# Keys and queries stored by class, the first norm's sums by parts, and halves for the last five output tiles

## The chip, the core and the metric

The kernel runs on one core of a Trainium2 chip. The core has five engines with queues of their own, and each runs its instructions in the order of its queue: TensorE (PE in the profile, PEld for its weight loads), VectorE (DVE), ScalarE (ACT), GpSimd (POOL) and SyncE (SP), which here issues nearly all DMAs. Semaphores are all that ties the queues together. TensorE writes to PSUM (8 banks of 128x512 f32); the other operands lie in SBUF.

The metric is the device time of one execution in microseconds; the median of three runs stands for a kernel.

## The reference

One decoder block over 512 tokens of width 1024, in float32. A vector `c` gives nine modulation vectors (shift, scale and gate for each of three sub-layers); around a token-mixing layer stand two feed-forward layers, and an RMSNorm ends it.

```python
mod = cond @ w_ada[l] + b_ada[l]                  # cond = silu(c), nine parts of 1024
u = modulate(rmsnorm(h, g_norm_ffn1[l]), sh1, sc1)
h = h + 0.5 * gt1 * swiglu(u, w_ffn1_in[l], w_ffn1_out[l])
u = modulate(rmsnorm(h, g_norm_mix[l]), sh2, sc2)
h = h + gt2 * token_mixing(u, cos, sin, w_in[l], w_pool[l], ...)
u = modulate(rmsnorm(h, g_norm_ffn2[l]), sh3, sc3)
h = h + 0.5 * gt3 * swiglu(u, w_ffn2_in[l], w_ffn2_out[l])
return rmsnorm(h, g_final)

def swiglu(u, w_in, w_out):                       # inner width 2816
    a, b = jnp.split(u @ w_in, 2, axis=-1)
    return (jax.nn.silu(a) * b) @ w_out

def token_mixing(u, cos, sin, w_in, ...):
    p, q, k, v, gate_logits = jnp.split(u @ w_in, cuts, axis=-1)
    y_pool = multiscale_pool(p, w_pool, pool_scale)
    q, k = apply_rope(q, ...), apply_rope(k, ...)  # 12 heads of 64, in 3 groups
    for gi, (window, dilation) in enumerate(((128, 1), (512, 4), (2048, 16))):
        o, lse = dilated_window_attention(q[gi], k[gi], v[gi], window // dilation, dilation)
    y_attn = sum of the groups' o, weighted by softmax of their lse
    merged = g_pool * (y_pool @ w_pool_branch) + g_attn * (y_attn @ w_attn_branch)
    return merged @ w_out
```

With dilation 4, token t attends to t, t - 4, t - 8 and so on: the tokens fall into four classes (t modulo 4) of 128 tokens, and queries meet only keys of their class. With dilation 16 the kernel uses the same four classes and a mask.

## The kernel before

Activations lie transposed: eight tiles `H[k]` of 128 channels x 512 tokens. A matmul of full float32 accuracy is made of three in the faster type fp32r (`mm3`, L321): weights and activations are each split into a high and a low part, and hi·uh, hi·ul and lo·uh are summed into one bank. Plain f32 matmuls, which the profile shows as two records each, serve for sums, spreads, scores and transposes.

Weights come by a list that is planned ahead (`plan`): SyncE loads chunks of 128x1024 or less into three buffers `raw` (in part of the run also `X`); `split_hi` (L257) writes the high half of a chunk to the ring `whi` on ScalarE (L280), `split_lo` (L286) the low half to `wlo` on VectorE (L292), and frees the buffer. `look(ahead)` (L301) splits so many chunks ahead of the one in use, `take` hands out the next. While `held` is set, `look` does nothing and chunks are split one by one. All queues are in the order of the Python program (`manual_schedule`).

The modulation is worked out on VectorE: `ada_fetch` loads a 128x1024 tile of `w_ada`, and `ada_do` (L341) multiplies it with `cond` and sums along the row into one column of `mod` (L346). `bg` does one such tile beside a piece of TensorE's work, and `bg_fetch` loads `ada_depth` tiles ahead.

The stages, in order:

- `startup` (L1336): loads, cond, squares of `H[k]` on ScalarE (L1369) summed pairwise into two tiles by VectorE (L1371), then across channels by one-column matmuls (L1377), root (L1378), reciprocal (L1381), and a spread of the result over 128 partitions by matmuls with the identity (L1386). `warm` (L1362) issues matmuls whose results are not used. `norm_t` (L420), `norm_u` (L427) and `norm_b` (L443) make a norm's scaled tile, its high part UH and its low part UL. Then the first four pairs of feed-forward 1, all eight k, in eight banks (L1421 to L1425).
- `ffn` (L788): pairs of tiles in and silu, or two pairs at once with seven products instead of eight (`duo`), and the output matrix in five parts. In the last part each output tile m gets its residual update (L856) and its squares (`sumsq`, added on GpSimd, L396). In feed-forward 1 the rotary tables' steps (`trig`, L888) are taken from `todo`, four for each m; the last step runs the sines on ScalarE (L912 to L914).
- `out_tail` (L475) does the last tiles of feed-forward 1 (m = 4 to 7) and of the mixing layer (m = 5 to 7) by halves A and B of 256 tokens: all tiles for A, then all for B. During B, `stats_t` (L398, L406) and `spread` (L413, L416) finish A's norm, and `norm_steps` gives the next stage's UH and UL, so that `head` can start on A.
- `mix` (L1113): projections, rotary embedding (`rope`, L918: four products of 128x512, L924, four add/subtracts of 64x512, L928 and L929), attention in units (kind, n, pair of heads). `at_prep` (L958) makes zero-padded queries for two heads, `at_scores` the scores (L975 and L977 for dilation 1, L981 for a class), the maximum on VectorE (L993) and Exp on ScalarE (L998), `at_turn` the transposes (L1010), `at_values` the values (L1033). `hooks` places these pieces between the k steps of projections. `pool_diff` is GpSimd's.
- `merge_out` (L1230): per m, two gate projections with four `bg`, then the merge of the branches into MH and ML (L1258 to L1262); then w_out.
- `ffn2`, and `out_end` (L514): the last five tiles in two parts of 384 and 128 tokens, with the final norm's statistics, products (`final`, L528, on VectorE and GpSimd) and stores (L531).

Classes are taken by a step of four in the free dimension:

```python
return ((0,), slice(n * P, n * P + P)) if kind == 0 else ((1, 2), slice(n, T, 4))
```

Of the kernel before, what the change touches and what calls it, by code (L numbers as in the profile page):

```python
# [136 lines left out]
class Kernel:  # L137
# [203 lines left out]
    def ada_do(self, j, n=1):  # L341
        t, mod = self.adat.pop(j), self.mod[:, j:j + 1]
        for i in range(n):
# [4 lines left out]
            if i:  # L348
                self.nc.vector.tensor_tensor(mod, mod, o, op=OP.add)
        if self.ada_free is not None:  # L350
            self.ada_free.append(t)
# [75 lines left out]
    def norm_u(self, n, k, hs, t):  # L427
# [3 lines left out]
        if n == 0:  # L431
            u = self.Xall.rearrange("p (a h k t) -> p a h k t", a=2, h=2, k=4)[:, k // 4, :, k % 4, :]
            act(u, t.rearrange("p (h t) -> p h t", h=2), AF.Identity, bias=S, scale=1.0)
# [41 lines left out]
    def out_tail(self, ms, ksrc, gate, nxt, squares):  # L475
# [7 lines left out]
        for h, hs in enumerate((A, Bh)):  # L483
            for m in ms:
# [10 lines left out]
                for i, (hi, lo, uh, ul) in enumerate(ks):  # L495
                    if h == 1 and m == ms[1] and i == 3:
                        self.stats_t(self.B[6], A)
                    if h == 1 and m == ms[2] and i == 1:
                        self.spread(self.B[6], A)
                        self.place_u(nxt)  # L500
                        step = self.norm_steps(nxt, A)
                    self.mm3(bank[:, hs], hi, lo, uh[:, hs], ul[:, hs], i == 0, i == len(ks) - 1)
                s = squares(m)[:, :HT]
                self.tail_step(m, hs, bank, gate, s)
                self.split_lo()
                if h == 1:
                    self.held = starts[m + 1]
                    if step:
                        step(1 if m != ms[-1] else 3)
                nc.vector.tensor_tensor(self.acc[:, hs], self.acc[:, hs], s, op=OP.add)  # L510
# [3 lines left out]
    def out_end(self, ms, ksrc, gate):  # L514
# [3 lines left out]
        M = nc.tensor.matmul  # L518
        tiles = {}
        A, Bh = slice(0, 3 * P), slice(3 * P, T)  # L520
# [12 lines left out]
        rA, rB = self.B[6], self.B[7]  # L533
        for h, hs in enumerate((A, Bh)):
            for m in ms:
# [6 lines left out]
                if h and m == ms[2]:  # L542
                    self.stats_t(rA, A)
                if h and m == ms[-1]:
                    self.spread(rA, A)
                    nc.scalar.activation(self.R[:, A], rA[:, A], AF.Copy)
                    for i in range(4):
                        final(g, i, A, self.R)
                        if i % 2:
                            store(i - 1, i + 1, A, nc.sync)  # L550
                    final(v, 4, A, rA)
                for i, (hi, lo, uh, ul) in enumerate(tiles[m]):
                    self.mm3(bank[:, hs], hi, lo, uh[:, hs], ul[:, hs], i == 0, i == len(tiles[m]) - 1)
                s = self.tp.tile([P, T], F32, name="ut")[:, :hs.stop - hs.start]
# [6 lines left out]
        self.stats_t(rB, Bh, (self.acc[:, Bh], s), lambda: final(v, 5, A, rA))  # L561
        scaled(ms[-1], Bh)
        store(4, 6, A, nc.scalar)
        self.spread(rB, Bh)
        for i in (6, 7):
# [925 lines left out]
```

## Time and profile before

| | us |
|---|---|
| three runs: median (lowest, highest) | 1047.0 (1045.74, 1047.56) |
| the profiled execution | 1041.36 |
| its span, first to last instruction | 1039.5 |
| TensorE idle within the span | 19.2 |
| from TensorE's last tile matmul to the end of the span | 9.8 |

Granted clock 0.995 on average. The span cut into 40 equal slices, in tenths of busy time (page, part 2):

```profile
PE   8999999999999999999999999999999999999996
DVE  6968879789786777777356677467787777667753
ACT  5443253525434543333324233453356254353542
PEclk9999999999999999999999999999999999999998
DMA  8857356455524223222044775421344234251202
```

TensorE has work in every slice. VectorE follows with some 7 tenths; where it drops, around the attention and at the end, TensorE is not waiting for it. DMA is heavy at the start and where the modulation is loaded. A busy TensorE says nothing of how fast its matmuls follow each other: the groups by line do. Means are of durations, which overlap; the distance between starts is what counts.

```profile
L683 PE MATMUL bank<-UH,whi 128*128 128x256 f32 x512 | 141.6, 277 | 0.0
L292 DVE TENSOR_TENSOR wlo<-raw,whi 128x1024 fp32r<-128x1024 f32 (+2 forms) x150 | 177.7, 1188 | 65.3 <-ACT whi L280 65.0
```

The columns: line, engine, operation, out<-in with the shapes, count | busy us, mean ns of one | idle time before, and what ended most of it.

### The profile page before, as it was taken

The numbers are of one execution on the slowest core, as the hardware profiler recorded it, in microseconds if no ns is written. First come the engines' busy times: TensorE is split into PE (matmuls) and PEld (weight loads), VectorE is DVE, ScalarE is ACT, GpSimd is POOL, SyncE is SP. The second block draws the span as 40 slices with busy tenths as digits, with TensorE's granted clock in tenths as the row PEclk, the third lists the DMA queues.
The fourth block names the chain that finished last, engine by engine and source line by source line (L and its number), as shares of the span: only waits on it lengthen the run. The fifth ranks groups of instructions, "written<-read, shape, count | busy, mean of one in ns | idle before, by whom it ended". The sixth has DMA issues, their size and how long they took to land.

```text
span 1039.5 us, 15505 instructions
## 1 busy us (share of the span) xinstructions
PE 1020.3 (98%) x6346; PEld 920.2 (89%) x6346; DVE 747.4 (72%) x1073; ACT 435.9 (42%) x635; POOL 37.6 (4%) x37
## 2 busy tenths in 40 slices
PE   8999999999999999999999999999999999999996
PEld 6888898989899899889988887998899899998996
DVE  6968879789786777777356677467787777667753
ACT  5443253525434543333324233453356254353542
POOL 0000000000000100008000000100000000000001
PEclk9999999999999999999999999999999999999998
DMA  8857356455524223222044775421344234251202
GB/s 309 283 203 242 123 202 200 164 165 174 169 71 132 91 76 102 62 61 82 11 157 158 229 237 197 130 61 61 102 152 133 80 102 142 82 157 61 93 16 82
DMA packets 42505, 139.14 MB, mean 134 GB/s; under 512 B 4673, under 2 KB 7617, under 8 KB 42434
## 3 DMA queue, kind: packets, MB, share of 16 engines
q1 hardware_dynamic: 41490, 137.42, 40.8%
q8 instruction: 50, 0.82, 0.3%
q10 hardware_dynamic: 944, 0.72, 0.2%
q14 instruction: 21, 0.17, 0.1%
HBM read 135.49 MB, written 2.64 MB: 133 GB/s over the span
## 4 chain that ended last, share of the span: by engine, by line
PE 84%; DVE 7%; DMA 3%; ACT 3%; issue 2%; SPq 0%; DVEq 0%; ACTq 0%
PE bank L325 14%; PE bank L324 14%; PE bank L323 14%; PE bank L683 10%; PE bank L685 10%; PE bank L684 10%; DMA ada<-wada 3%; DVE ada L346 2%; DVE wlo L292 1%; PE bank L1421 1%; PE bank L1425 1%; PE bank L1423 1%; PE bank L981 1%; PE bank L1033 1%; PE bank L1212 1%
## 5 line engine op out<-in xcount | busy, mean ns | idle before, releaser
L292 DVE TENSOR_TENSOR wlo<-raw,whi 128x1024 fp32r<-128x1024 f32 (+2 forms) x150 | 177.7, 1188 | 65.3 <-ACT whi L280 65.0
L280 ACT ACTIVATE whi<-raw 128x1024 fp32r<-128x1024 f32 (+2 forms) x150 | 150.3, 1008 | 49.4 <-DVE raw L228 36.9
L323 PE MATMUL bank<-UH,whi 128*128 128x512 f32 (+1 forms) x432 | 159.3, 369 | 2.0 <-ACT UH L430 2.0
L324 PE MATMUL bank<-UL,whi 128*128 128x512 f32 (+1 forms) x432 | 155.1, 359 | 0.3
L325 PE MATMUL bank<-UH,wlo 128*128 128x512 f32 (+1 forms) x432 | 154.9, 359 | 0.2 <-DVE wlo L292 0.2
L325 PE MATMUL bank<-HI,wlo 128*128 128x512 f32 (+3 forms) x406 | 147.9, 364 | 0.4 <-DVE wlo L292 0.4
L323 PE MATMUL bank<-HI,whi 128*128 128x512 f32 (+3 forms) x406 | 148.0, 364 | 0.0
L324 PE MATMUL bank<-HK,whi 128*128 128x512 f32 (+3 forms) x406 | 147.8, 364 | 0.0
L683 PE MATMUL bank<-UH,whi 128*128 128x256 f32 x512 | 141.6, 277 | 0.0
L684 PE MATMUL bank<-UL,whi 128*128 128x256 f32 x512 | 141.6, 277 | 0.0
L685 PE MATMUL bank<-UH,wlo 128*128 128x256 f32 x512 | 141.6, 277 | 0.0
L292 DVE TENSOR_TENSOR wlo<-X,whi 128x1024 fp32r<-128x1024 f32 (+1 forms) x87 | 104.4, 1200 | 43.7 <-ACT whi L280 43.5
L683 PE MATMUL bank<-SH,whi 128*128 128x256 f32 x384 | 107.0, 279 | 0.0
L685 PE MATMUL bank<-SH,wlo 128*128 128x256 f32 x384 | 106.9, 278 | 0.0
L684 PE MATMUL bank<-SL,whi 128*128 128x256 f32 x384 | 106.9, 278 | 0.0
L280 ACT ACTIVATE whi<-X 128x1024 fp32r<-128x1024 f32 (+1 forms) x87 | 89.2, 1037 | 29.2 <-DVE X L228 27.4
L683 PEld LDWEIGHTS bank<-UH,whi 128*128 128x128 f32 x512 | 96.1, 188 | 0.3
L684 PEld LDWEIGHTS bank<-UL,whi 128*128 128x128 f32 x512 | 96.1, 188 | 0.3
L685 PEld LDWEIGHTS bank<-UH,wlo 128*128 128x128 f32 x512 | 96.4, 188 | 0.0
L323 PEld LDWEIGHTS bank<-UH,whi 128*128 128x128 f32 x432 | 81.4, 188 | 14.4 <-ACT UH L430 2.4
L325 PEld LDWEIGHTS bank<-UH,wlo 128*128 128x128 f32 x432 | 81.3, 188 | 13.3 <-DVE wlo L292 0.6
L324 PEld LDWEIGHTS bank<-UL,whi 128*128 128x128 f32 x432 | 81.4, 189 | 12.7 <-DVE UL L445 0.7
(222 smaller groups left out, 1752.9 us busy)
## 6 DMA issues: line engine op xcount, KB each, us to landing
ada<-wada SPq DMA_DIRECT2D x47, 512.0 KB, 4.7
raw<-wmix SPq DMA_DIRECT2D x44, 512.0 KB, 3.8
raw<-wf1i SPq DMA_DIRECT2D x34, 512.0 KB, 4.5
raw<-wf2i SPq DMA_DIRECT2D x30, 512.0 KB, 3.5
X<-wf2i SPq DMA_DIRECT2D x14, 512.0 KB, 3.5
cs<-wada SPq DMA_DIRECT2D x12, 512.0 KB, 3.5
AR<-wada SPq DMA_DIRECT2D x12, 512.0 KB, 4.4
raw<-wf2o SPq DMA_DIRECT2D x12, 512.0 KB, 4.0
```

The costliest lines, as they stand in the source:

```text
L280: self.nc.scalar.activation(self.hi[:, y], r[:, x], AF.Copy)
L292: self.nc.vector.tensor_tensor(self.lo[:, y], r[:, x], self.hi[:, y], op=OP.subtract)
L323: M(ps, hi, uh, start=start, stop=False)
L324: M(ps, hi, ul, start=False, stop=False)
L325: M(ps, lo, uh, start=False, stop=stop)
L346: self.nc.vector.scalar_tensor_tensor(t[:, c], t[:, c], 1.0, self.cond[:, c], op0=OP.mult, op1=OP.mult, accum_out=o)
L683: M(o, hi, uh, start=start and p == 0 and k == 0, stop=False, skip_group_check=True)
L684: M(o, hi, ul, start=False, stop=False, skip_group_check=True)
L685: M(o, lo, uh, start=False, stop=k == 3, skip_group_check=True)
L981: M(S[:, o + i * P:o + i * P + P], qz[:, (2 * i + h) * P:(2 * i + h + 1) * P], k[:, toks], start=True, stop=True)
L1033: M(o, pt[:, blk * P:blk * P + P], v, start=i == 0, stop=i == len(srcs) - 1)
L1212: M(b, self.UH[k][:, c::4], hi, start=k == 0, stop=False)
```

## The change

Six edits in one:

1. `rope` gets `classes`: with 4 it writes its results by class, reading the products with step 4; `at_tokens` then takes a contiguous block for dilations 4 and 16 too.
2. `startup`: the squares' sums go into one-column matmuls in three parts (k odd up to 5, k even up to 6, k = 7 alone), the reciprocal stands between the two halves of modulation tile 8, the first weight chunk's high half and UH stand ahead of the copy of the spread, and the warm-ups are other ones. The constants' load moves behind tile 8's.
3. `out_end`: halves of 256 tokens instead of 384 and 128; products and stores are placed anew.
4. `out_tail`: the first norm step right behind the spread, and the low half of a split behind the steps.
5. `ffn`, last part: `look` up to five chunks ahead instead of three, and six trig steps for each m instead of four.
6. `merge_out`: four modulation buffers instead of two, loaded four ahead.

```diff
@@ -338,7 +338,7 @@
         self.adat[j] = t
-    def ada_do(self, j, n=1):
+    def ada_do(self, j, n=1, between=None):
         t, mod = self.adat.pop(j), self.mod[:, j:j + 1]
@@ -347,6 +347,8 @@
                 self.nc.vector.tensor_tensor(mod, mod, o, op=OP.add)
+            elif between:
+                between()
         if self.ada_free is not None:
@@ -424,13 +426,17 @@
         return t
-    def norm_u(self, n, k, hs, t):
+    def norm_x(self, k, hs, t):
+        u = self.Xall.rearrange("p (a h k t) -> p a h k t", a=2, h=2, k=4)[:, k // 4, :, k % 4, :]
+        self.nc.scalar.activation(u, t.rearrange("p (h t) -> p h t", h=2), AF.Identity, bias=self.mod[:, k:k + 1], scale=1.0)
+    def norm_u(self, n, k, hs, t, rest=True):
         S = self.mod[:, 24 * n + k:24 * n + k + 1]
...
         act(self.UH[k][:, hs], t[:, hs], AF.Identity, bias=S, scale=1.0)
-        if n == 0:
-            u = self.Xall.rearrange("p (a h k t) -> p a h k t", a=2, h=2, k=4)[:, k // 4, :, k % 4, :]
-            act(u, t.rearrange("p (h t) -> p h t", h=2), AF.Identity, bias=S, scale=1.0)
+        if n == 0 and rest:
+            self.norm_x(k, hs, t)
         if n == 2 and hs.start:
@@ -499,14 +505,15 @@
                         step = self.norm_steps(nxt, A)
+                        step(0)
                     self.mm3(bank[:, hs], hi, lo, uh[:, hs], ul[:, hs], i == 0, i == len(ks) - 1)
...
                 self.tail_step(m, hs, bank, gate, s)
-                self.split_lo()
                 if h == 1:
...
                         step(1 if m != ms[-1] else 3)
+                self.split_lo()
                 nc.vector.tensor_tensor(self.acc[:, hs], self.acc[:, hs], s, op=OP.add)
@@ -515,9 +522,9 @@
         v, g = nc.vector, nc.gpsimd
-        M = nc.tensor.matmul
         tiles = {}
-        A, Bh = slice(0, 3 * P), slice(3 * P, T)
+        A, Bh = slice(0, HT), slice(HT, T)
+        rA, rB = self.B[6], self.B[7]
         self.held = self.pos
@@ -539,36 +545,39 @@
                         nc.scalar.preload_act_table(AF.Sqrt)
-                if h and m == ms[2]:
-                    self.stats_t(rA, A)
-                if h and m == ms[-1]:
-                    self.spread(rA, A)
-                    nc.scalar.activation(self.R[:, A], rA[:, A], AF.Copy)
-                    for i in range(4):
-                        final(g, i, A, self.R)
-                        if i % 2:
-                            store(i - 1, i + 1, A, nc.sync)
-                    final(v, 4, A, rA)
+                n = len(tiles[m])
                 for i, (hi, lo, uh, ul) in enumerate(tiles[m]):
-                    self.mm3(bank[:, hs], hi, lo, uh[:, hs], ul[:, hs], i == 0, i == len(tiles[m]) - 1)
-                s = self.tp.tile([P, T], F32, name="ut")[:, :hs.stop - hs.start]
+                    if h and m == ms[1] and i == n // 2:
+                        self.stats_t(rA, A)
+                    if h and m == ms[2] and i == n // 2:
+                        self.spread(rA, A)
+                        nc.scalar.activation(self.R[:, A], rA[:, A], AF.Copy)
+                        for j in range(4):
+                            final(g, j, A, self.R)
+                            if j % 2:
+                                store(j - 1, j + 1, A, nc.sync)
+                    self.mm3(bank[:, hs], hi, lo, uh[:, hs], ul[:, hs], i == 0, i == n - 1)
+                s = self.tp.tile([P, T], F32, name="ut")[:, :HT]
                 self.tail_step(m, hs, bank, gate, s)
...
                 v.tensor_tensor(self.acc[:, hs], self.acc[:, hs], s, op=OP.add)
-        self.stats_t(rB, Bh, (self.acc[:, Bh], s), lambda: final(v, 5, A, rA))
+                if h and m in ms[2:4]:
+                    j = 4 + 2 * (m - ms[2])
+                    for x in (j, j + 1):
+                        final(v, x, A, rA)
+                    store(j, j + 2, A, nc.sync)
+        self.stats_t(rB, Bh, (self.acc[:, Bh], s))
         scaled(ms[-1], Bh)
-        store(4, 6, A, nc.scalar)
         self.spread(rB, Bh)
-        for i in (6, 7):
-            final(v, i, A, rA)
-        store(6, 8, A, nc.sync)
-        for i in range(KT):
-            final(v, i, Bh, rB)
-            if i in (2, 5, 7):
-                store({2: 0, 5: 3, 7: 6}[i], i + 1, Bh, nc.sync if i == 5 else nc.scalar)
+        nc.scalar.activation(self.R[:, Bh], rB[:, Bh], AF.Copy)
+        for e, js, queue in ((v, (0, 1), nc.scalar), (g, (2, 3), nc.sync), (v, (4, 5), nc.scalar), (v, (6, 7), nc.scalar)):
+            for j in js:
+                final(e, j, Bh, rB if e is v else self.R)
+            store(js[0], js[1] + 1, Bh, queue)
     def head(self, n, banks, table):
@@ -833,7 +842,7 @@
             def ks(m):
-                self.look()
+                self.look(max(3, min(m + 2, 5)))
                 return [(hi, lo, *hk[k]) for k, (hi, lo) in enumerate(self.take())]
@@ -857,7 +866,7 @@
                     nc.scalar.activation(self.O[m], self.H[m], AF.Copy, scale=self.g(3)[:, m:m + 1])
-                for _ in range(4):
+                for _ in range(6):
                     if self.todo:
@@ -915,7 +924,8 @@
         return todo
-    def rope(self, pa, pb, dst):
+    def rope(self, pa, pb, dst, classes=1):
         v = self.nc.vector
@@ -925,8 +935,10 @@
             cols = slice(T * half, T * half + T)
-            v.tensor_tensor(dst[0:64, cols], t[0][rows], t[1][rows], op=OP.subtract)
-            v.tensor_tensor(dst[64:128, cols], t[2][rows], t[3][rows], op=OP.add)
+            src = [x[rows].rearrange("p (i c) -> p c i", c=classes) for x in t]
+            to = [dst[r, cols].rearrange("p (c i) -> p c i", c=classes) for r in (slice(0, 64), slice(64, 128))]
+            v.tensor_tensor(to[0], src[0], src[1], op=OP.subtract)
+            v.tensor_tensor(to[1], src[2], src[3], op=OP.add)
     def mm_tile(self, hooks=()):
@@ -943,9 +955,10 @@
         kind, n, hp = u
-        return ((0,), slice(n * P, n * P + P)) if kind == 0 else ((1, 2), slice(n, T, 4))
+        return (1, 2) if kind else (0,), slice(n * P, n * P + P)
     def at_prep(self, u):
@@ -1192,7 +1205,7 @@
                     ps = [self.mm_tile(hooks(todo.pop(0), nxt=todo[0] if todo else ())) for s in range(2)]
-                    self.rope(ps[0], ps[1], dst)
+                    self.rope(ps[0], ps[1], dst, 4)
             g23 = [[(1, c, hp) for hp in range(2)] for c in range(4)]
@@ -1231,10 +1244,10 @@
         with tc.tile_pool(name="mb", bufs=1) as mb, tc.tile_pool(name="mw", bufs=6) as mw, \
-                tc.tile_pool(name="mada", bufs=2) as self.adaw:
+                tc.tile_pool(name="mada", bufs=4) as self.adaw:
             MH = [mb.tile([P, T], F32R, name=f"MH{k}") for k in range(KT)]
             ML = [mb.tile([P, T], F32R, name=f"ML{k}") for k in range(KT)]
-            self.ada_stop, self.ada_depth = 72, 2
+            self.ada_stop, self.ada_depth = 72, 4
             self.bg_fetch()
@@ -1344,8 +1357,8 @@
         nc.sync.dma_start(self.vecs, a["vecs"])
+        self.ada_fetch(8, 2)
         nc.sync.dma_start(self.cst, a["cst"][:, :163])
-        self.ada_fetch(8, 2)
         self.fetch(0)
@@ -1361,31 +1374,39 @@
                 M(self.B[5][:, :P], self.ones, x[:, :P], start=True, stop=True)
+        def part(s, first, last):
+            for n in range(4):
+                M(self.B[7][:, n:n + 1], s[:, n * P:(n + 1) * P], self.ones[:, 0:1], start=first and n == 0, stop=last,
+                  skip_group_check=True)
         acc = (self.acc, self.R)
...
             nc.scalar.activation(s, self.H[k], AF.Square)
-            if k > 1:
+            if 1 < k < 7:
                 v.tensor_tensor(acc[k % 2], acc[k % 2], s, op=OP.add)
-            if k < 7:
-                warm(1, self.H[min(k, 3)])
-        for n in range(4):
-            for i in range(2):
-                M(self.B[7][:, n:n + 1], acc[i][:, n * P:(n + 1) * P], self.ones[:, 0:1], start=i == 0, stop=i == 1)
+            if k < 4:
+                warm(2 if k > 1 else 1, self.H[k])
+            elif k in (5, 6):
+                part(acc[k % 2], k == 5, False)
+            elif k == 7:
+                part(s, False, True)
         nc.scalar.activation(self.r4, self.B[7][:, :4], AF.Sqrt, bias=self.eps, scale=1.0 / D)
+        warm(2, self.H[7])
+        g, b1 = self.g(0), self.vecs[:, 8:16]
         self.ada_do(0)
-        self.ada_fin("shift", 0, 1)
-        v.reciprocal(self.r4, self.r4)
-        g, b1 = self.g(0), self.vecs[:, 8:16]
-        v.scalar_tensor_tensor(b1, b1, 1.0, g, op0=OP.add, op1=OP.mult)
+        self.ada_do(8, 2, lambda: v.reciprocal(self.r4, self.r4))
         for n in range(4):
             M(self.B[6][:, n * P:(n + 1) * P], self.r4[:, n:n + 1].to_broadcast([P, P]), self.ident, start=True, stop=True)
-        warm(10, self.acc)
-        self.ada_do(8, 2)
+        warm(6, self.H[7])
+        v.scalar_tensor_tensor(b1, b1, 1.0, g, op0=OP.add, op1=OP.mult)
+        self.ada_fin("shift", 0, 1)
         def scale(k):
@@ -1395,15 +1416,19 @@
         self.Rn = {0: self.B[6]}
+        self.split_hi()
         t = self.norm_t(0, 0, full)
+        self.norm_u(0, 0, full, t, rest=False)
+        self.ada_do(1)
+        self.norm_b(0, 0, full, t)
+        self.split_lo()
         nc.scalar.activation(self.R, self.B[6], AF.Copy)
         self.Rn[0] = self.R
-        self.split(0)
-        self.norm_u(0, 0, full, t)
-        self.norm_b(0, 0, full, t)
+        self.norm_x(0, full, t)
         for k in range(KT):
             if k + 1 < KT:
-                self.ada_do(k + 1)
+                if k:
+                    self.ada_do(k + 1)
                 self.ada_fin("shift", k + 1, k + 2)
```

## What I predicted

> **What bounds the kernel now.** I read the page, then TensorE's waits, then the timeline of each place where TensorE waits or runs thin, then the granted clock by windows.
>
> ```profile
> PE 1020.3 (98%) x6346; PEld 920.2 (89%) x6346; DVE 747.4 (72%) x1073; ACT 435.9 (42%) x635; POOL 37.6 (4%) x37
> ```
>
> TensorE is busy for all but 19.2 of 1039.5 us. So time can come from two sources only: those 19.2 us (start 0 to 7, end 1029.7 to 1039.5, and a few waits), and matmuls that take longer than they need. The waits (us in total, times, longest):
>
> ```profile
> PE bank L323 <- ACT UH L430: 2.0, 2, 1.5
> PE bank L323 <- ACT MH L1261: 1.4, 1, 1.4
> PE bank L406 <- DVE AR L510: 1.1, 1, 1.1
> ```
>
> The slow matmuls, in TensorE's timeline (start, us, what): four records of contiguous keys, and eight of keys taken with step 4.
>
> ```profile
> 407.43 0.60 PE L975 MATMUL bank<-k,qz 128*128 128x128 f32 x4
> 407.79 0.48 PE L323 MATMUL bank<-UH,whi 128*128 128x512 f32 x1
> ...
> 482.60 2.00 PE L981 MATMUL bank<-k,qz 128*128 128x128 f32 x8
> 484.24 0.60 PE L1212 MATMUL bank<-whi,UH 128*128 128x512 f32 x1
> ```
>
> The starts inside such groups stand 0.110 us apart at L975 and 0.227 at L981, the same 128 columns each. The next lines are stretches of the run: busy time of PE, PEld, DVE, ACT and POOL, and then the granted clock (1.00, then 0.50), the DMA's share and GB/s.
>
> ```profile
> 10.97:14.38 3.41, 2.48 (x19) 2.31 (x20) 2.60 (x8) 0.26 (x1) 0.00 (x0) 1.00 1.05 392
> 14.38:17.80 3.42, 3.42 (x19) 3.42 (x18) 2.03 (x8) 1.21 (x3) 0.00 (x0) 0.50 1.04 413
> 359.10:362.50 3.40, 2.25 (x20) 2.08 (x19) 2.35 (x6) 0.99 (x3) 0.00 (x0) 1.00 0.75 196
> ```
>
> A stretch of 3.41 us with mostly one-column matmuls (L1377) was followed by one at half clock; a stretch with 2.25 us of ordinary matmuls was not.
>
> **The change part by part.** Profiled execution: 1041.36 us, span 1039.5. I sum differences and take them from the median of the runs, 1047.0; the profiled one lies 5.6 below it, and I assume the difference stays.
>
> *Keys and queries by class.* The 8 units of L981 lose their step. Now a unit costs: first record 482.60 to next matmul 484.24 is 1.64, and that matmul then holds TensorE 0.44 instead of 0.235, so 1.84. Contiguous: two groups like L975's (0.36 + 0.31 - 0.23 = 0.44 each), 0.88. Eight units: 8 x 0.95 = 7.6 gained. What pays: `rope` reads its products with step 4 in 16 add/subtracts of 64x512 (0.69 each now). The nearest row is the query preparation L958: pitch 0.20 contiguous, 0.245 with step 4 (2.06 for 8), so 0.045 more per 128 elements, 0.18 for 512 with one such input, 0.36 with two: 0.7 to 1.4 per rope. Behind the rope on VectorE stands a unit's maximum, then ScalarE's Exp, then TensorE's transposes; at 455.4 these start about 1.0 us after they could. So 0 to 0.4 shows at each of three ropes. And preparation L958 under GpSimd's work took 4.15 for 8 (489.20), ending 1.4 before its scores; GpSimd would now overlap all of it: 0 to 0.8. I take 0.5 off: **-7.1** (-7.7 to -5.5).
>
> *Startup.* Now: last square 10.80, add 11.67, 16 one-column records to 13.45, root, reciprocal 13.78, spread 14.01 to 15.77, ten warm-ups to 18.89, and L1421 starts there (UH was ready at 18.84). Changed: three parts, 24 records at 0.112, from 10.5 (add of k=5 ends 10.46): 2.7 plus two at half clock gives 13.5. So the parts alone gain nothing: the eight records more eat the earlier start. The modulation half that now stands ahead of the reciprocal (0.68) fits between 12.3 and 13.45. The gain is later: ScalarE no longer has the copy of R (0.50) and the weight's first half (1.04) between norm and UH, and 6 warm-ups replace 10. Spread 14.1; if the clock falls at 14.38 again, spread ends 15.8, norm 16.75, UH 17.5, but twelve warm-up records (ten at 0.214, two at 0.112) end at 18.1. If it does not fall, UH is ready at 16.9. Gain 0.8 or 2.0; the window would again hold mostly one-column matmuls, so I take **-0.9** (-2.0 to -0.3). The next k is covered: VectorE needs 5.32 per k, TensorE 5.6. The constants' DMA moves behind two halves of a modulation tile (0.5 MB, 1.3 us at the 400 GB/s of that time) and lands near 13.2, ahead of the spread.
>
> *Norm behind the spread, first place (feed-forward 1 to mixing).* UH's wait at 367.61 (0.48, and 0.17 of slow first matmul) goes: -0.65. But the other two edits here work on the same engines.
>
> ```profile
> 346.78 0.64 ACT L912 ACTIVATE cs<-cs 128x512 f32<-128x512 f32 x1 [0.43 <-DVE cs L908]
> 349.46 0.96 DVE L292 TENSOR_TENSOR wlo<-X,whi 128x768 fp32r<-128x768 f32 x1 [2.71 <-ACT whi L280]
> 350.34 0.74 DVE L856 SCALAR_TENSOR_TENSOR H<-bank,mod,H 128x512 f32<-128x512 f32 x1
> 360.06 0.41 DVE L510 TENSOR_TENSOR AR<-AR,X 128x256 f32<-128x256 f32 x1
> 360.62 0.58 PE L406 MATMUL bank<-ones,AR 128*128 128x1 f32 x4 [1.15 <-DVE AR L510]
> ```
>
> Now one weight half (341.24) passes ahead of the sines; taking six trig steps at a time puts the sines ahead of it, and `look(4)`, `look(5)` then put two splits ahead of each of the updates L856 of m=2 and m=3. Played through with these durations: trig ends 344.4 to 345.0, sines leave ScalarE at 346.2 to 346.9, two splits, update 2 ends 349.5 to 350.2, its square, two splits (one 1024 wide), update 3 ends 353.7 to 354.9 (now 351.0), square, table load 1.28, and the first half-tile's square only at 356.0 to 356.8 (now 353.8). From there 1.9 per tile: the sum for L406 is ready at 361.6 to 362.9 instead of 360.47. TensorE loses its 0.39 wait for wlo at 354.06 and so stands there from 358.7: 3 to 4 us idle, +1.6 net. After such an idle stretch the clock would fall for 3.41 us, 1.7 more, taken at 1.5. Sum **+2.4** (-2.5 if the sum came in time, to +4). [...]
>
> *Deeper modulation buffers.*
>
> ```profile
> 634.84 1.22 DVE L346 SCALAR_TENSOR_TENSOR ada<-ada,cond 128x1024 f32<-128x1024 f32 x1 [1.50 <-DMA ada<-wada]
> 640.25 0.50 PE L323 MATMUL bank<-MH,whi 128*128 128x512 f32 x1 [1.45 <-ACT MH L1261]
> ```
>
> Per m, VectorE has 10.7 us of work (four modulation tiles 5.0, splits 3.1, gates 2.6) beside TensorE's 14.0, and waits 2.8 for DMA: it ends late, and TensorE's matmuls of 638.42 to 641.31 take 2.9 instead of 0.7. With four buffers the DMA's 5 us lie a whole m ahead, the last MH is ready near 632. SyncE still waits for the same release before each tile, with weight loads queued behind; VectorE being earlier, they go earlier. Two more tiles (1 MB) at 537 fall in an empty stretch of the queue to 544. **-2.2** (-2.3 to -0.5).
>
> *Norm behind the spread, second place.*
>
> ```profile
> 683.78 0.38 PE L323 MATMUL bank<-UH,whi 128*128 128x256 f32 x1 [1.51 <-ACT UH L430]
> ```
>
> Here the steps stood behind the last tile; now three of 0.4 run at 681.0 to 682.3 inside it, and UL of k=0 and k=1 come 0.1 and 0.35 late. 1.9 - 0.4: **-1.5** (-1.9 to -0.4).
>
> *Last five tiles.* 90 matmuls of 384 columns at 0.174 and 90 of 128 at 0.112 become 180 of 256, 0.1195 in the same place of both other tails: 90 x (0.174 + 0.112 - 0.239) = 4.2. Sums and spread of the first part go from 6 records to 4 each: 0.4. After the last matmul: update, square, four more one-column records, two more spread records, six VectorE products at 0.33 instead of eight at 0.20: 5.4 instead of 4.2 to the last product. But the DMAs end it: all 2 MB go out from 1031.3 to 1037.7.
>
> ```profile
> 1036.00:1037.00 1.00, 0.00 (x0) 0.00 (x0) 0.00 (x0) 0.00 (x0) 0.00 (x0) 0.50 0.99 287
> ```
>
> With halves 1 MB leaves before the last matmul, and the other takes 3 us from 4.9 after it: 8 us, as now (8.2). Tail 0 (-1 to +1.5). **-4.5** (-5.3 to -3).
>
> Sum: -7.1 - 0.9 + 2.4 - 2.2 - 1.5 - 4.5 = -13.8: 1033.2 us.
>
> **Rivals.** (a) The tail of feed-forward 1 comes in time: GpSimd disturbs VectorE less, or the two splits taken early pay back. For it: four splits beside the half tiles become three. Against: the table load stands behind update 3 in both. -13.8 - 2.4 - 2.5: 1028.3. (b) The scores' gain is swallowed (L958 under GpSimd's work, or the transposes). For: the 1.43 us that one L958 took at 491.68. Against: slack of 1.0 to 1.4 at both. 1047.0 - 6.7 = 1040.3. (c) Slower: `rope` with step 4 holds VectorE. With x more per add/subtract three ropes stall 4x - 1.0 each; the sign turns at 12x - 3 = 13.8, x = 1.4, that is 2.1 us instead of 0.69. At four times 0.69, x = 2.07: 3 x 7.3 and 3 at the fourth, 25: 1058. Against: L958's 0.045. [...] (d) The changed parts do what they say but the clock, the DMAs or the output give it back: no change, 1047.
>
> **How the numbers follow.** Forecast 0.63, (a) 0.21, (b) 0.08, (c) 0.05, (d) 0.03. All bounds at once give 1025.3 and 1041.3; the range 1026 to 1040 holds the forecast with most of its bounds, and (a); (b) lies at its edge. Differences under 0.2% (2 us) a measurement of this kernel can't tell from none. Faster: 0.63 + 0.21 + 0.08 = 0.92; same 0.02, slower 0.06 from (c), (d).
>
> **What would show it.** L981's records 0.11 apart; first real matmul at 18.1 or near 17; a longer wait of L406 for AR (3 us) with a half clock behind it, or none, (a); no wait for MH or UH; last matmul 4 to 5 us earlier against the stage before, the end 9 to 10 us behind it; `rope`'s add/subtract under 1.1 us. Wrong if those groups stay at 0.22, or if VectorE's waits move to the transposes.

## The result, and the profile after

| | before | after |
|---|---|---|
| median of 4 runs, us | 1046.37 (1045.30 to 1047.56) | 1032.93 (1032.45 to 1033.83) |
| ratio, 95% interval | | 0.9872 (0.9855 to 0.9889) |
| profiled execution, us (span) | 1041.36 (1039.5) | 1033.15 (1031.4) |

The changed kernel is 1.3% faster, 13.4 us by the medians; 1033.2 was forecast, counted from 1047.0, the median of the first three runs of the kernel before. The two profiled executions differ by only 8.2 us. The profile of the kernel before lies 5.0 under its own median, the one of the changed kernel on it, although the prediction assumed that this distance would stay.

Placed by TensorE's first instruction of each stage, the 8.1 us between the two spans are made of these pieces (after minus before):

| stretch | us | the prediction's step |
|---|---|---|
| start to first main matmul (18.89 to 20.05) | +1.2 | startup, -0.9 |
| last part of feed-forward 1 to the mixing head's first matmul | +5.1 | tail of feed-forward 1, +2.4 |
| mixing head's first matmul to the first score group | -0.8 | (norm steps, first place) |
| first to last score group | -5.9 | classes, -7.1 |
| w_out (first MH matmul to feed-forward 2) | -3.9 | buffers -2.2, second tail -1.5 |
| last five tiles | -4.5 | -4.5 |
| last matmul of a weight to the end of the span | +0.5 | 0 |

The stretches between them moved by 0.2 or less. Now the lines themselves. The longest of TensorE's waits behind the startup (us in total, times, longest):

```profile
PE bank L408 <- DVE AR L517: 4.6, 1, 4.6
```

The waits for UH and MH are gone. The wait of the norm's sums for AR, 1.15 before, is 4.6 now. The timeline of TensorE shows that wait, and further on a score group of a class (start, us, what):

```profile
364.76 0.98 PE L408 MATMUL bank<-ones,AR 128*128 128x1 f32 x4 [4.63 <-DVE AR L517]
...
478.58 1.05 PE L994 MATMUL bank<-k,qz 128*128 128x128 f32 x8
```

The eight records of a class take 1.05 us where they took 2.00, and start 0.11 us apart, as those of L975 did before: contiguous keys pay nothing extra. What pays for it is `rope`, in VectorE's groups (busy us, mean ns):

```profile
L941 DVE TENSOR_TENSOR q<-rt,rt 64x512 f32<-64x512 f32 x6 | 5.7, 951 | 0.1
```

0.951 instead of 0.687: 0.26 for each of 16 add/subtracts, within the forecast's 0.18 to 0.36. The wait of 4.6 us did not come alone. By windows, around it (PE, PEld, DVE, ACT, POOL, then the granted clock):

```profile
360.62:364.03 3.41, 0.00 (x0) 0.00 (x0) 3.02 (x6) 1.25 (x3) 0.00 (x0) 1.00 0.45 151
364.03:367.44 3.41, 2.68 (x12) 2.71 (x13) 1.42 (x4) 0.80 (x3) 0.00 (x0) 0.50 0.50 156
367.44:370.85 3.41, 3.41 (x18) 3.41 (x17) 2.18 (x5) 2.27 (x4) 0.00 (x0) 0.50 0.00 0
```

One stretch of 3.41 us is empty, and the next two run at half clock: the first of them, with 0.73 us still idle and 0.84 us of one-column sums, was followed by 0.50 once more. The forecast had 3 to 4 us of wait and one stretch at half clock.

Two questions were left for the chip. Which of the two edits in this tail makes the sum late? And why did the total come out when the profile shows three steps worse than forecast (startup, tail and classes)?

### The profile page after: what moved, and what is told of

Its sections match the earlier page's. It is cut to its first block, busy times and chain, and to the rows that moved or that the text cites. A ratio compares the mean times of both kernels' runs of the same rounds, so it can differ in the third digit from the quotient of the medians.

```text
span 1031.4 us, 15497 instructions
## 1 busy us (share of the span) xinstructions
PE 1013.7 (98%) x6350; PEld 915.8 (89%) x6350; DVE 752.0 (73%) x1070; ACT 435.8 (42%) x636; POOL 38.2 (4%) x39
## 4 chain that ended last, share of the span: by engine, by line
PE 93%; DVE 4%; ACT 1%; issue 1%; DMA 0%; SPq 0%; DVEq 0%; ACTq 0%
PE bank L323 17%; PE bank L325 17%; PE bank L324 17%; PE bank L692 10%; PE bank L694 10%; PE bank L693 10%; PE bank L1446 1%; PE bank L1448 1%; PE bank L1450 1%; PE bank L1046 1%; PE bank L1225 1%; PE bank L1226 1%; PE bank L1227 1%; DVE wlo L292 1%; PE bank L994 1%
## 5 line engine op out<-in xcount | busy, mean ns | idle before, releaser
L323 PE MATMUL bank<-HI,whi 128*128 128x512 f32 (+1 forms) x406 | 147.9, 364 | 0.0
L325 PE MATMUL bank<-HI,wlo 128*128 128x512 f32 (+1 forms) x406 | 147.4, 363 | 0.0
L324 PE MATMUL bank<-HK,whi 128*128 128x512 f32 (+1 forms) x406 | 147.4, 363 | 0.0
```

The source lines that it names most:

```text
L323: M(ps, hi, uh, start=start, stop=False)
L324: M(ps, hi, ul, start=False, stop=False)
L325: M(ps, lo, uh, start=False, stop=stop)
```

## The experiments

Unless said otherwise, a kernel is the changed one with one edit, run four to six times. The sets of runs below were taken on three chips. The one changed version that was run in two of them gave 1027.54 twice; the kernel before gave medians of 1046.4, 1046.9, 1043.8 and 1048.3 in four sets. Differences below are of medians, and across sets those under some 3 us rest on the profiles beside them: as ratios to the kernel before of the same set, 0.9851 (0.9823 to 0.9879) for pops_undone and 0.9851 (0.9822 to 0.9880) for look_undone overlap the changed kernel's 0.9872 (0.9855 to 0.9889).

**before_again**: no edit.

> The kernel before, once more. Its profiled execution of 1041.36 us lies 5.0 below the median of its runs, 1046.37; the changed kernel's profiled one lies on its median. Theory: an execution of the kernel before differs from another by how often the granted clock falls (one stretch of 3.41 us at half clock costs 1.7), so a profile near 1046 shows about three such stretches more than the one near 1041, at the startup or at the waits of TensorE. Rival: the 5 us are spread evenly over the run (memory, or a clock somewhat lower throughout), and no single place shows them.

Ten runs: 1041.1 to 1050.6, median 1045.57; seventeen runs beside it 1042.7 to 1049.95. Its profile (1045.2) is 3.8 us longer than the first in span, and two places hold all of it: the first main matmul stands at 21.74 instead of 18.89 (+2.85), and w_out takes 0.9 more, with the wait for MH at 2.3 instead of 1.4. In this execution the granted clock first rose at 21.88 us; in the first profile it rose at 10.97, fell at 14.38 for 3.41 us and rose again. The rival falls, since two places hold the difference. Of the theory only the places hold: what I named as three stretches was one late rise, and one longer wait at which the clock did not fall.

**tail_undone**: both scheduling edits in the last part of feed-forward 1.

```diff
-                self.look(max(3, min(m + 2, 5)))
+                self.look()
-                for _ in range(6):
+                for _ in range(4):
```

> The changed kernel with four trig steps and the splits as before in the last part of feed-forward 1 (norm steps behind the spread are kept). Theory: the 4.6 us wait of the sums for AR and the two half-clock stretches behind it come from these two edits. The wait goes back to about 1.2 us, the clock stays up, and the mixing head starts about 5.5 us earlier: 0.0047 to 0.0062 of the time less than the changed kernel (1026.5 to 1028). Rival: the norm steps moved ahead of split_lo and the add of the squares make AR late; then the wait stays above 3 us and the time is the changed kernel's within 1 us.

1027.54 us (1025.0 to 1028.2), 0.9816 (0.9794 to 0.9837) of the kernel before, and 5.4 less than the changed kernel. TensorE's wait for AR in its profile:

```profile
PE bank L408 <- DVE AR L517: 1.2, 1, 1.2
```

and the clock stays up:

```profile
361.02:364.44 3.42, 2.69 (x23) 2.72 (x24) 1.96 (x6) 0.89 (x3) 0.00 (x0) 1.00 0.78 241
```

The mixing head starts 5.8 us earlier. The moved norm steps are not the cause: they are still there.

**pops_undone** and **look_undone**: one line each of the diff above.

> The changed kernel with four trig steps per update instead of six, the splits taken early as in the change. Undoing both gave 5.4 us less than the changed kernel (wait for AR 1.2 us instead of 4.6). Theory: the early splits are what makes the sum late (two splits of 0.83 and 0.95 us ahead of each of the updates of m=2 and m=3, where one stood), and the trig steps only shift VectorE's own work: with four steps the wait is still above 3 us and the time within 1.5 us of the changed kernel. Rival: the six steps make it late (they hold the updates back by up to 1.4 us); then the wait goes to about 1.2 us and the time to 1027 to 1029.

> The changed kernel with the splits taken as before, six trig steps kept. Theory (early splits are the cause): the wait for AR is 1.2 to 2 us, the clock stays up behind it, and the time is 1026.5 to 1029. Rival (six steps are the cause): wait above 3 us, time within 1.5 us of the changed kernel. If each alone brings the wait down, the two only do harm together.

1029.40 (1028.2 to 1030.2) and 1029.47 (1027.9 to 1032.1): each is 3.5 us better than the changed kernel and 1.9 worse than both undone. The profiles agree: from the first matmul of the last pairs of feed-forward 1 to the mixing head it is 47.65 us in the changed kernel, 44.33 and 44.11 here, and 41.95 with both undone. Neither theory holds as a whole (of look_undone's the wait and the clock came true, the time missed its 1029 by 0.5); each edit does harm of its own. With the early splits alone the wait for AR is 2.6, and one stretch at half clock follows:

```profile
359.66:363.07 3.41, 0.77 (x7) 0.73 (x7) 2.42 (x5) 1.02 (x4) 0.00 (x0) 1.00 0.80 239
363.07:366.49 3.42, 3.42 (x18) 3.42 (x18) 1.50 (x5) 1.21 (x4) 0.00 (x0) 0.50 0.17 68
```

With the six steps alone the wait for AR is 1.2 and the clock stays up, but TensorE waits 2.2 us for low halves, twice 1.01:

```profile
PE bank L325 <- DVE wlo L292: 2.2, 3, 1.0
```

Taken together the two queue up on ScalarE and VectorE until AR is 4.6 us late.

**start_undone**: `startup` as in the kernel before.

> The changed kernel with the startup of the kernel before. Theory: the granted clock stayed at half until 19.28 us in the changed kernel because the six warm-ups and the one-column records leave TensorE too idle for the clock to rise near 11 us; with the old startup the clock rises at 10.97, falls for 3.41 us at 14.38, and the first main matmul starts at 18.9 instead of 20.05: 1.2 us less than the changed kernel. Rival: the position of the clock's windows is set by chance from execution to execution, and the mean gain is nothing (within 0.5 us) or has the other sign.

1033.39 (1033.0 to 1034.3): 0.5 more than the changed kernel, not clear of the spread of either, so the rival's "within 0.5, or the other sign" is right and my reading of the two profiles was wrong. Its first main matmul stands at 20.47, behind a late rise: its 16 one-column sums took 3.75 us, as in before_again; in the first profile 14 of the 16 took 1.72. The 18.89 of the first profile was not the old startup's time but that of an early rise. The changed startup shows both cases too. One execution of tail_undone (1027.54), late rise at 19.70:

```profile
20.02 1.18 PE L1446 MATMUL bank<-UH,whi 128*128 128x512 f32 x4
```

and one of **tail_undone_2**, the same kernel once more, with the clock up at 9.99:

```profile
17.43 0.94 PE L1446 MATMUL bank<-UH,whi 128*128 128x512 f32 x3
```

> The kernel tail_undone once more, as the common base of the three runs sent with it: 0.9816 of the kernel before, within 0.002.

1027.54 again (1024.99 to 1027.9), 0.9802 (0.9781 to 0.9822). Its profiled execution is its fastest: the 2.5 us between it and the others are the 2.6 us of this startup. The mean granted clock leaves out the time before the first rise (0.995 in the first profile of the kernel before: 3.41 us at half behind 14.38 and 7.94 at the end, of the 1028.6 us behind the rise at 10.97), and so it tells the two cases apart: the runs at 1025.0 of both sets have 0.995, the other seven 0.997 or 0.998. Early rise against early rise the new startup gains 1.5 (18.89 to 17.43). Late against late a gain can't be told: 20.47 and 21.74 with the old one, 19.8 to 21.4 with the new.

**att_undone**: attention by step 4 as before.

```diff
-                    self.rope(ps[0], ps[1], dst, 4)
+                    self.rope(ps[0], ps[1], dst)
-        return (1, 2) if kind else (0,), slice(n * P, n * P + P)
+        return ((0,), slice(n * P, n * P + P)) if kind == 0 else ((1, 2), slice(n, T, 4))
```

> The changed kernel with rope and at_tokens as before (keys and queries of the second and third group read with step 4). Theory: each of the eight units costs 1.84 us of TensorE instead of 0.88, less some 0.5 to 1.0 that the strided add/subtracts of rope (0.95 us instead of 0.69, 16 of them) bring back: 6.0 to 7.1 us more than the changed kernel. Rival: rope's longer instructions cost more on the path than 1.1 us (three ropes at up to 1.06 each show whole) and the gain is 4.5 or less.

1039.31 (1036.7 to 1039.5): 6.4 more. From the first to the last score group its profile has 103.64 us, the changed kernel's 97.77.

**rope_plain**, on tail_undone: `rope` without classes, `at_tokens` as changed.

> tail_undone with rope's add/subtracts reading contiguous again, while the scores still take contiguous blocks (so keys and queries of groups 2 and 3 are attended in blocks instead of by class, and the rest is computed on that). It shows what the step-4 reads of rope cost: they are 0.95 us each instead of 0.69, 1.06 per rope. The attention stage gained 5.87 us in the profiles where 7.1 were forecast. Theory: the missing 1.2 us are rope's, and this kernel's stage (first to last score group) is 1.0 to 1.4 us shorter than the 97.7 of tail_undone. Rival: rope hides wholly, the stage stays within 0.3 us of 97.7, and the eight units gained less than 0.95 us each.

1026.50 (1023.95 to 1028.5) beside 1027.54: no difference that the medians can tell. In the profiles the stage is 96.85 us against 97.76, so 0.9 of `rope`'s 3 x 1.06 us shows, between the two theories. Some 0.7 of it stands at one place, where transposes (L1023, at 422.85 in tail_undone_2) wait for Exp. That splits the 5.9: units 103.64 - 96.85 = 6.8 (8 x 0.95 forecast), less 0.9 for `rope` (0.5 forecast). Set side by side, the profiles of rope_plain and of the kernel before give 0.93 for each of two units, as forecast, and 0.83 for the other six: behind those stands L1225 (L1212 before), which still holds TensorE 0.44.

**mada_undone**: two modulation buffers in the mixing.

```diff
-                tc.tile_pool(name="mada", bufs=4) as self.adaw:
+                tc.tile_pool(name="mada", bufs=2) as self.adaw:
-            self.ada_stop, self.ada_depth = 72, 4
+            self.ada_stop, self.ada_depth = 72, 2
```

> The changed kernel with two modulation buffers in the mixing as before. Runs of the kernel before spread over 1041 to 1051 us, those of the changed kernel over 1032.4 to 1033.9, and two profiles of the kernel before show the wait for MH at 1.4 and 2.3 us. Theory: with two buffers each tile's load starts late and its landing decides the mixing's length, which differs from execution to execution; so the runs spread over 5 us or more and the median is 3 to 7 us above the changed kernel, more than the 2.3 to 3.2 us that the profiles show. Rival: the spread of the kernel before comes from its startup's clock alone; then these runs spread by less than 2.5 us and lie 2 to 3 us above the changed kernel.

1035.32, from 1033.4 to 1040.0: 2.4 more at the median, and a spread of 6.5 us where the changed kernel has 1.4. The spread is the theory's; the median misses its 3 to 7 and lies in the rival's 2 to 3; and as a ratio, 0.9912 (0.9882 to 0.9942), it overlaps the changed kernel's. Its profile (1040.0) shows how one execution loses 6.8, 6.7 of them in w_out. The chain of waits, DVE's timeline behind it, and TensorE by windows:

```profile
630.30 6.09 DMA ada<-wada
```

```profile
636.48 1.23 DVE L346 SCALAR_TENSOR_TENSOR ada<-ada,cond 128x1024 f32<-128x1024 f32 x1 [2.47 <-DMA ada<-wada]
```

```profile
636.48:639.90 3.42, 1.43 (x7) 0.85 (x5) 3.35 (x7) 0.00 (x0) 0.00 (x0) 1.00 0.17 68
639.90:643.31 3.41, 1.43 (x3) 0.90 (x4) 2.43 (x4) 1.57 (x2) 0.00 (x0) 0.50 0.47 154
643.31:646.72 3.41, 3.41 (x10) 2.63 (x9) 2.68 (x5) 0.73 (x2) 0.00 (x0) 0.50 0.44 147
```

A tile of `w_ada` lands 6.1 us after its buffer came free, MH is 4.0 late instead of 1.4, and two stretches at half clock follow.

**order_undone**, on tail_undone: `step(0)` taken out and `split_lo` put back ahead of the steps in `out_tail`.

> tail_undone with the norm steps of both out_tail places where they stood in the kernel before (the first one not right behind the spread, the others behind split_lo). Theory: the waits for UH come back at both places: 0.5 to 0.65 us at the mixing head and 1.5 to 1.7 at feed-forward 2, together 2.0 to 2.4 us more than tail_undone. Rival: norm steps that stand earlier only take VectorE's time from the last splits, and the difference is under 1 us.

1032.31 (1032.1 to 1033.1): 4.8 more than tail_undone, twice what I expected. The waits for UH came back as priced: 0.6 at the mixing head, where 0.6 more was lost before the first scores, and 1.67 at feed-forward 2. But the second one now drags the clock down, which it had not done in either profile of the kernel before:

```profile
676.78 0.38 PE L323 MATMUL bank<-UH,whi 128*128 128x256 f32 x1 [1.51 <-ACT UH L437]
```

```profile
673.95:677.36 3.41, 1.77 (x14) 1.36 (x12) 1.88 (x6) 1.29 (x3) 0.00 (x0) 1.00 0.41 156
677.36:680.77 3.41, 3.41 (x16) 3.41 (x17) 3.41 (x10) 1.92 (x4) 0.00 (x0) 0.50 0.02 5
```

Feed-forward 2 is 1.4 us longer by it. The last 0.5 stands behind the last matmul of a weight, and what put it there is open.

**end_undone**: `out_end` with 384 and 128 columns as before.

> The changed kernel with the last five tiles in 384 and 128 columns and their output as before. Theory: 90 matmuls of 384 and 90 of 128 columns take 4.5 us more than 180 of 256, and the tail behind the last matmul 0.5 less: 4.0 us more than the changed kernel (3.5 to 4.5). Rival: the output's DMAs end the run in either; then the difference is under 2 us.

1037.23 (1034.4 to 1037.8): 4.3 more. In the profile the last five tiles take 26.85 us instead of 22.34, and the rest to the end 10.2 instead of 10.7: the theory, both terms.

**early_warm**, on tail_undone: a startup of my own (the copies of the conditioning vector also go behind the squares).

```diff
+        warm(12, self.ones)
         for i in range(2):
             M(self.B[i], self.ones[0:1, :], self.cond[0:1, i * T:(i + 1) * T], start=True, stop=True)
...
-            if k < 4:
-                warm(2 if k > 1 else 1, self.H[k])
+            if k == 0:
+                warm(6, self.ones)
             elif k in (5, 6):
                 part(acc[k % 2], k == 5, False)
+                warm(1, self.ones)
```

> tail_undone with another startup: twelve warm-ups on the constant ones as soon as these are written (1.0 us), then the two matmuls of the conditioning vector, six more warm-ups, and one behind each of the first two parts of the norm; the conditioning vector's copies stand behind the squares. Theory: the startup is priced by the clock. In five profiles of the changed startup it stayed at half until 18.3 to 21.3 us, and the 24 one-column records took 5.1 us instead of 2.7. With TensorE busy from 1.0 us on, the clock is up by 8 us at the latest, the parts end near 13.2, and the first main matmul starts at 16 to 17.5 instead of 20: 2.5 to 4 us less than tail_undone. Rival: the startup is bound by the landing of weights and modulation, so that the first matmul comes earlier but the eight k behind it wait for data and the end of the section stays: less than 1 us.

1028.33 (1025.5 to 1029.0), 0.9809 (0.9788 to 0.9831): no gain over tail_undone. The clock did rise early (at 7.07; the 8 us ahead of the run was an estimate), and the first main matmul came at 17.87, 2.15 before the late-rise case and 0.4 behind the early one. The stretch from there to the last pairs of feed-forward 1 took the same 306.1 us as in the other runs, so the rival's mechanism (data that lands late) falls, though its "less than 1 us" came true. The profiled execution (1025.48) keeps these 2.15; the clock, which fell again, kept them from being more:

```profile
10.48:13.90 3.42, 3.42 (x32) 3.41 (x31) 2.83 (x7) 1.06 (x3) 0.00 (x0) 1.00 1.05 384
13.90:17.31 3.41, 3.41 (x17) 3.22 (x16) 2.32 (x9) 1.58 (x3) 0.00 (x0) 0.50 1.04 416
```

TensorE counts as busy throughout the first line, mostly with one-column matmuls, and the clock falls behind it. The other three runs have mean granted clocks of 0.991 to 0.992 against 0.995 in this one: 0.003 to 0.004 of 1027 us, at a loss of half, is 6 to 8 us more at half clock, worth 3 to 4 us, and they are 2.5 to 3.5 longer. So the clock seems to have taken the gain back; where those stretches lie is not known, since those runs left no trace.

The best version is thus tail_undone: the change without its two edits in the last part of feed-forward 1, 1027.5 us, 1.8 to 2.0% under the kernel before.

## Why the prediction came out

The total was right (1033.2 for 1032.93), the sign and the mechanisms were right, and two terms were each about 2.5 us too small, with opposite signs. That the total came out to 0.3 us is luck in good part: the sum of -13.8 was worked out on a profile, and against that profile the changed kernel's is only 8.2 us shorter. The 5.6 us that the sum had too much are about the 5.0 by which the profile of the kernel before lay under its median. Each step of the sum against the run that undoes it (medians):

| step | forecast | measured |
|---|---|---|
| keys and queries by class | -7.1 | -6.4 |
| startup | -0.9 | -0.5 (not clear of the spread) |
| trig by six and early splits (+2.4, and the 0.65 of UH) | +3.05 | +5.4 |
| norm steps behind the spread, both places (-0.65 - 1.5) | -2.15 | -4.8 (on tail_undone) |
| modulation buffers | -2.2 | -2.4 |
| last five tiles | -4.5 | -4.3 |
| sum | -13.8 | -13.0 (both kernels: -13.4) |

*Classes.* Right, as 6.8 - 0.9 rather than 8 x 0.95 - 0.5. My two groups of four contiguous keys fit two units; in the other six the matmul behind the scores costs its 0.44 with contiguous keys too, 0.1 each that I had counted as gained. And 0.4 us more of `rope` reached the path. Rival (b), gain swallowed, and rival (c), `rope` as the bound, needed 6.7 us lost and 1.4 us more per add/subtract; 0.9 and 0.26 were measured. Nor did VectorE pay for the step what TensorE's scores had paid: 0.951 to 0.687 is a factor of 1.38, 0.227 to 0.110 one of 2.06.

*Startup.* The first matmul was put at 18.1, or 16.9 if the clock stayed up: measured 17.4 with an early rise, and there the clock did fall again (at 13.40). What the forecast missed is that the old 18.89 was itself the early case, and that the clock mostly rises late: in eight of ten profiles with the changed startup, where the first matmul came at 19.8 to 21.4 (early_warm has one of its own), and in two of three with the old one (20.5 and 21.7).

*Tail of feed-forward 1.* The step "3 to 4 us idle, +1.6 net", with one stretch of 3.41 us at half clock, was the right mechanism, mis-sized: 4.6 us idle, and two stretches. Update 3 ended at 356.4. The whole tail stands 1.2 us later than in the profile of before (338.66 against 337.48 at its first update), so that is 355.3 beside the forecast's 353.7 to 354.9; update 2 was as late against its latest time already. VectorE's two splits between the updates took 2.70 us, the first 1.49 instead of the 0.96 that I played through, while GpSimd worked beside it (1.48 in the profile of before too). The sum was ready 0.7 past the forecast's latest time. The larger part of what was missing is the second stretch at half clock. The 1.5 us for a clock that falls behind an idle stretch were an estimate: the rows ahead of it show that fall behind a stretch of mostly one-column matmuls (2.48 of 3.41 us, then 0.50), none behind an idle one. The empty stretch at 360.62 with 0.50 behind it is the first row here that shows it. Rival (a), the sum in time, falls.

*Norm steps.* The step "1.9 - 0.4: -1.5" priced the wait and left out what follows it. Order_undone shows 1.67 for the wait and another 1.4 for the half clock behind it, and at the first place 1.2 where 0.65 stood. In the profile of before the same 1.5 us had cost no clock: they fell across the border of two stretches, with 2.3 and 2.9 us of matmuls left in these. In before_again (mean clock 0.996) it stayed up behind a wait of 1.5 us for UH too. I took that outcome for the rule.

*Modulation buffers.* Right at the median, for the reason given (a DMA that lands late). The change did more than shorten that wait: it took a wait away whose length differs from run to run (for MH 1.4 and 2.3 us in the two profiles of the kernel before, 4.0 in mada_undone's).

*The assumption that the profile stays 5.6 under the median* is the step that failed outright. Executions of the kernel before lie between 1041 and 1051 because of three things, as far as the record shows: the startup's clock (2.85 between its two profiles), the landing of modulation tiles, and, as order_undone suggests, the half clock behind the wait for UH. The change removes the last two, so its runs lie close together, and the median gained more than the first profile could show. That those two waits make up the rest of the distance is shown one by one only where they are put back into the changed kernel; no run of the kernel before at 1049 left a trace. The recorded clocks point the same way: all nine of its runs at 1049 us or more have 0.991 on average, its two profiles 0.995 and 0.996, and 0.004 of 1047 us is some 8 us more at half clock, or 4 us of time.

## What to carry to other kernels

Price a wait of the busiest engine with what follows it: here a stall that left 1.77 us of matmuls in a stretch of 3.41 was followed by a stretch at half clock, one that left 1.97 was not, and such a stretch costs up to another 1.7 us, half its length (1.4 in order_undone). Read two or three profiles before a single one is taken as the baseline, since a kernel with such waits spreads over 1% and the profile may be its best case. An edit that pulls work forward on a loaded engine has to be tried alone: here two such edits cost 5.4 us of the 18.8 that the others gained.

## What the runs showed of the chip

- The clock behind a thin stretch of 3.41 us, as measured: stretches with 0.00 (changed kernel, 360.62), 0.77 (pops_undone, 359.66), 1.43 (mada_undone, 636.48) and 1.77 us of matmuls (order_undone, 673.95) were followed by 0.50, those with 1.97 (before, 639.02 to 642.44, at the wait for MH), 2.25 (before, 359.10), 2.30 (before, 679.97) and 2.69 (tail_undone, 361.02) by 1.00. So in these runs 1.64 us without a matmul in one stretch were enough, and 1.45 were not.
- Stretches that were busy mostly with one-column matmuls did not keep the clock up: 3.42 of 3.42 us (early_warm, 10.48) was followed by 0.50, and so was 2.48 of 3.41 (before, 10.97). At the end of the kernel before (1028.14) 2.19 of 3.42, 0.71 of them one-column sums, was followed by 0.50 too. The 2.68 behind the long wait of the changed kernel (364.03), 0.84 of them one-column sums and all at half clock, did not bring the clock back.
- The borders of these stretches stood elsewhere in each execution profiled. The same kernel rose at 9.99 us in one and at 19.70 in another, and the first main matmul moved by 2.6 us with it (17.43 and 20.02). The rises at 9.99, 19.28 (changed kernel) and 19.70 us, in three executions with the same startup, are not whole stretches of 3.41 us apart.
